# The first feed-forward product of a hybrid decoder by Strassen's algorithm, its result kept in fp32

## The chip, the cores and the metric

The kernel runs on one core of a Trainium2 chip, in one launch. The metric is the device time of that core in microseconds (us), the median over several executions. The engines are named as in the profile: PE (TensorE, matmuls), PEld (its weight loads), DVE (VectorE), ACT (ScalarE), POOL (GpSimd) and SP (SyncE, which issues the DMAs).

## The reference

One inference step of a decoder with two layers, D = 1024 features, over 576 tokens (512 of a prompt and 8 sequences of 8). Each layer is

```
x <- LN(alpha*x + 0.5*SwiGLU_1(x))
x <- LN(alpha*x + W_out(gated sum of four mixing branches of x))
x <- LN(alpha*x + 0.5*SwiGLU_2(x))
SwiGLU(x): gate, up = split(x @ w_in); (silu(gate) * up) @ w_out
```

`w_in` is 1024 x 4096 (2048 gate columns, 2048 up columns) and `w_out` 2048 x 1024, all in fp32. There are four feed-forward layers (FFN), two in each layer. The four branches (RWKV, pooling, gated delta rule, attention into a memory) and their states lie between the two FFNs of a layer; the change doesn't touch them.

## The kernel before, in words

**Numbers.** Every dense product is done in three passes: an fp32 operand is split into a high part (a cast to fp32r) and a low part (the difference). A weight piece of 128 x 4 x 128 comes by a DMA of 256 KB into `raw`, ACT casts it into `w[:, 0]` (line 232), DVE subtracts into `w[:, 1]` (line 234); `unit` does this for a piece of n x 128 rows. x, h and the like are split by `split` (lines 261 and 262), in the same two steps. `mms` (line 248) issues for each 128 rows of the contraction high x high, high x low and low x high: three matmuls of 128x128 weights and 288 tokens.

**Tokens.** Features lie on the partitions, tokens along the free axis, in two halves of 288 (`HALVES`). x is held split, in eight tiles `X`.

**One FFN** (`ffn`): 16 blocks j of 128 hidden columns. A block takes two units of weights (gate, up) and, for each half s, two products of 8 x 3 = 24 matmuls into PSUM (`pg`, `pu`); then ACT makes silu(gate), DVE multiplies by up (line 433), and `split` writes the result as `H[j]`. The second product (`out_norm`) runs over 8 output blocks with all 16 H, 48 matmuls a half, in pieces of 4 x 3 matmuls; the second half of the tokens follows the first 3 pieces behind, and the first half does the last 8 pieces at once. Then comes the residual (DVE, line 281, onto T_j, which POOL made from the two parts of x, line 274), the sums for the norm, and `layer_norm` in steps: a small chain on DVE, two products with ones (`prow`), and for each block a multiplication (DVE, line 352), an addition (POOL, line 353), scale and bias (ACT), and the split into X. The first half's norm lies beside the end of the second half's products; the second half's norm (`finish_norm`) is left to what follows, and the next FFN does three blocks of the first half meanwhile.

**The mixing's output product** goes through `out_norm` as well, with 8 operand tiles instead of 16: 24 matmuls for a block and half.

**Order.** The code is traced in Python and a scheduler places the instructions on each engine's queue by their order in the code and by when they can start; on the chip each engine runs its queue in order, and waits are semaphores. Tiles with the same tag share a fixed number of slots (`BUFS`): 8 of "x", 8 of "s", 4 of "d", 3 of "p", 2 of "iv", 4 of "w" and 4 of "wm" (weights), 3 and 3 for `raw`. PSUM has two banks for each of the tags "mm" and "mg" of these products.

Of the kernel before, what the change touches and what calls it, by code (L numbers as in the profile page):

```python
# [15 lines left out]
P = 128  # L16
# [3 lines left out]
NS = 8          # sample sequences  # L20
LS = 8          # tokens of each
# [4 lines left out]
NC_ = 9         # chunks of 64 tokens: 8 of the prompt, one of the sample group  # L26
# [24 lines left out]
# rows of 128 parameters, in two groups that one transpose each brings onto the partitions  # L51
# [5 lines left out]
# how the work that fills the tensor engine's gaps in the token mixing is laid between the rest: its order at first  # L57
# (P: pooling and attention, G: gates of the first merge), how many steps of it go where, and how many columns of an
# inverse lie between two steps
ORDER = "P" * 11 + "GP" * 16  # L60
PLAN = (12, 0, 4, 0, 12, 8, 0, 0, 2, 0, 4, 4, 0, 2)
RWKV_EVERY, DELTA_EVERY = 3, 8


class Decoder:
# [45 lines left out]
    def tri(self, t, strict, block=None):  # L111
        """t[s, j] (square in the last two dims of a [n, n] tile): 1 where s <= j (s < j if strict) else 0."""
# [5 lines left out]
    def blockdiag(self, t, b):  # L118
        """zero outside the b x b diagonal blocks of t [n, m]."""
# [8 lines left out]
    def constants(self):  # L128
# [11 lines left out]
        # inclusive upper triangles, by chunk of 64 and by sequence of 8  # L140
# [6 lines left out]
        # seqmask[t, b] = 1 where token t (mod 64) belongs to sequence b  # L147
# [3 lines left out]
        # masks of the RWKV token x token matrices [s | s, t strict | t inclusive]  # L151
# [10 lines left out]
        # 0 where s <= t else NEG: [128 = (h, s), 2 kinds, 64]  # L162
# [5 lines left out]
        # stacked identity [128 = (h, s), 64]  # L168
        self.id2 = c.tile([P, 64], F32, name="id2")
        nc.vector.tensor_add(self.id2, self.ident[:, 0:64], self.ident[:, 64:128])  # L170
        # rows 4 r + g of the identity on the partitions (.., g, 8 matrices): [128, 8, 32]
# [8 lines left out]
        # 0 at the first token of a chunk or sequence, else 1  # L180
# [6 lines left out]
        # 1 / (t + 1)  # L187
# [4 lines left out]
    def params(self, l):  # L192
        """parameters of a layer, feature on partition, one column for each block of 128."""
# [27 lines left out]
    def unit(self, src):  # L221
        """a [128, n, 128] piece of a weight, n <= 8, as high and low parts: tiles [128, 2, 4, 128]."""
# [28 lines left out]
    def stash(self, k, src, sl=slice(0, NT)):  # L251
        """rows k (of 14 blocks) of the branches' outputs, to DRAM."""
        dst = self.od[k][:, sl]
        if len(src.shape) == 3:
            dst = dst.rearrange("p (c t) -> p c t", t=src.shape[2])
        self.nc.sync.dma_start(dst, src)
# [1349 lines left out]
```

## Time and profile before

| | |
|---|---|
| median of three runs | 3292.2 us (3291.89 to 3294.51) |
| profiled execution, its span | 3291.1 us, 62683 instructions |
| the profiled execution's own time | not given beside the span |
| PE busy | 3164.5 us, 96%, 24736 matmuls |
| DVE busy | 1896.7 us, 58% |
| ACT busy | 1276.8 us, 39% |
| POOL busy | 581.2 us, 18% |
| DMA | 271.96 MB, mean 83 GB/s |

Busy time of PE is that of pipelined instructions, whose ends are modelled: 24 matmuls one behind the other show as one row that is a little longer than the distance to the next. The span's clock is 0.974 of the upper level in the mean. The four FFNs lie at about 22 to 337, 1325 to 1644, 1644 to 1960 and 2952 to 3269 us.

### The profile page before, as it was taken

How to read it: one execution, taken by the hardware profiler on the slowest of the kernel's cores; microseconds unless marked ns; L12 is line 12 of the kernel's file. 1: busy time of each engine (PE TensorE's matmuls, PEld its weight loads, DVE VectorE, ACT ScalarE, POOL GpSimd, SP SyncE). 2: the span in 40 equal slices, each digit the busy share in tenths (PEclk: the TensorE clock that was granted, in tenths of full speed). 3: DMA queues.
4: the chain of work that ended last, by engine and by line, in shares of the span. 5: the costliest groups of instructions: out<-in, count | busy, mean ns of one | idle time of the engine just before them, and what ended most of it. 6: DMA issues, size and time to landing. Idle time of an engine off the chain costs nothing. (4 is left out here: it accounts for less than half of the span.)

```text
span 3291.1 us, 62683 instructions
## 1 busy us (share of the span) xinstructions
PE 3164.5 (96%) x24736; PEld 2886.2 (88%) x24736; DVE 1896.7 (58%) x4205; ACT 1276.8 (39%) x3015; POOL 581.2 (18%) x898
## 2 busy tenths in 40 slices
PE   7999999999999999999999999998999999999998
PEld 7999887688888799999999998776888797989998
DVE  5336676465677656733663376675475786475336
ACT  4323544434434233432343244444345342343324
POOL 2002311111110014400330032111111100152004
PEclk8999899999999899999999999999999998999999
DMA  4223331142233233332333232312322232323222
GB/s 137 80 84 96 87 111 44 41 118 55 60 83 78 57 105 91 91 87 80 88 103 87 81 107 72 105 51 55 102 58 61 67 99 64 98 85 97 84 81 77
DMA packets 509908, 271.96 MB, mean 83 GB/s; under 512 B 45897, under 2 KB 500141, under 8 KB 509613
## 3 DMA queue, kind: packets, MB, share of 16 engines
q1 hardware_dynamic: 509612, 267.95, 29.0%
q8 instruction: 194, 3.18, 0.4%
q14 instruction: 102, 0.83, 0.1%
HBM read 248.12 MB, written 19.76 MB: 81 GB/s over the span
## 5 line engine op out<-in xcount | busy, mean ns | idle before, releaser
L234 DVE TENSOR_TENSOR w<-raw,w 128x512 fp32r<-128x512 f32 (+1 forms) x824 | 604.7, 739 | 385.2 <-ACT w L232 378.0
L232 ACT CAST w<-raw 128x512 fp32r<-128x512 f32 (+1 forms) x824 | 501.6, 615 | 608.8 <-PE po L248 236.4
L248 PE MATMUL pp<-X,w 128*128 128x288 f32 x3552 | 550.9, 307 | 11.1 <-DVE X L262 5.5
L248 PEld LDWEIGHTS pp<-X,w 128*128 128x128 f32 x3552 | 495.1, 193 | 40.1 <-issue 15.3
L248 PE MATMUL pgt<-X,w 128*128 128x288 f32 x3072 | 500.9, 309 | 5.1 <-ACT th__12080 L1484 2.1
L248 PEld LDWEIGHTS pgt<-X,w 128*128 128x128 f32 x3072 | 435.1, 193 | 32.6 <-issue 13.9
L248 PE MATMUL pg<-X,w 128*128 128x288 f32 x3072 | 441.8, 297 | 10.2 <-DVE X L262 6.1
L248 PE MATMUL pu<-X,w 128*128 128x288 f32 x3072 | 437.4, 297 | 0.0
L248 PEld LDWEIGHTS pg<-X,w 128*128 128x128 f32 x3072 | 419.7, 189 | 15.7 <-DVE X L262 9.6
L248 PEld LDWEIGHTS pu<-X,w 128*128 128x128 f32 x3072 | 420.9, 190 | 0.6
L248 PE MATMUL po<-H,w 128*128 128x288 f32 x3072 | 413.9, 296 | 0.0
L248 PEld LDWEIGHTS po<-H,w 128*128 128x128 f32 x3072 | 409.4, 188 | 1.3
L248 PE MATMUL pbr<-O,w 128*128 128x288 f32 x1344 | 227.6, 308 | 12.9 <-ACT w L232 4.1
L248 PEld LDWEIGHTS pbr<-O,w 128*128 128x128 f32 x1344 | 190.9, 191 | 27.9 <-issue 7.3
L276 POOL TENSOR_TENSOR T<-T,m 128x288 f32<-128x288 f32 x48 | 48.0, 1029 | 925.7 <-ACT m L297 925.4
L433 DVE TENSOR_TENSOR h<-h,pu 128x288 f32<-128x288 f32 x128 | 58.0, 453 | 259.2 <-PE pu L248 259.1
L261 ACT CAST H<-h 128x288 fp32r<-128x288 f32 x128 | 55.2, 431 | 189.5 <-DVE h L433 189.4
L432 ACT ACTIVATE h<-pg 128x288 f32<-128x288 f32 x128 | 52.7, 411 | 172.8 <-PE pg L248 172.8
L248 PE MATMUL po<-mh,w 128*128 128x288 f32 x768 | 109.0, 302 | 9.2 <-DVE T L281 9.2
L248 PEld LDWEIGHTS po<-mh,w 128*128 128x128 f32 x768 | 105.6, 193 | 11.4 <-DVE T L281 6.9
L614 DVE TENSOR_TENSOR it<-W,iu 128x60 f32<-128x60 f32 (+24 forms) x372 | 97.7, 263 | 9.2
L353 POOL TENSOR_TENSOR T<-T,off 128x288 f32<-128x288 f32 x96 | 83.4, 900 | 91.5 <-ACT off L348 65.0
(1018 smaller groups left out, 3747.8 us busy)
## 6 DMA issues: line engine op xcount, KB each, us to landing
raw<-in_w_in_dram SPq DMA_DIRECT2D x280, 256.0 KB
raw<-in_ffn_w_in_dram SPq DMA_DIRECT2D x272, 256.0 KB
raw<-in_ffn_w_out_dram SPq DMA_DIRECT2D x160, 256.0 KB
raw<-in_w_branch_dram SPq DMA_DIRECT2D x48, 256.0 KB
raw<-in_w_out_dram SPq DMA_DIRECT2D x48, 256.0 KB
oraw<-od SPq DMA_DIRECT2D x28, 288.0 KB
kraw<-in_mem_w_kv_dram SPq DMA_DIRECT2D x16, 256.0 KB
kvr<-in_cache_mem_k_dram SPq DMA_DIRECT2D x16, 256.0 KB
```

What stands on the lines that cost most here:

```text
L232: nc.scalar.copy(w[:, 0, :m], raw)
L234: low.tensor_sub(w[:, 1, :m], raw, w[:, 0, :m].bitcast(F32))
L248: self.nc.tensor.matmul(ps, w[:, wp, d, :], X[k][:, part, sl], start=first and k == 0 and q == 0, stop=last and k == n - 1 and q == 2)
L261: nc.scalar.copy(out[:, 0, sl], src)
L276: nc.gpsimd.tensor_sub(t, t, self.stat[s]['m'])
L353: nc.gpsimd.tensor_add(T[j], T[j], off)
L432: nc.scalar.activation(h, pg, AF.Silu)
L433: nc.vector.tensor_mul(h, h, pu)
L614: nc.vector.tensor_mul(w, d[:, :r, k:k + 1].to_broadcast([P, r, m]), u[:, k + 1:, k].unsqueeze(1).to_broadcast([P, r, m]))
```

## The change

The first product of each FFN is computed as a 2 x 2 block product with seven block products instead of eight (Winograd's form). The contraction is cut in two (four blocks of 128 features each), the tokens in their two halves (B11, B21: the first half's x; B22 and T1 to T4: the second half's x and differences of both), the columns in gate and up. `seven` makes the operands, as the layer norm (or `load_x`, at the start) delivers x: for the first half the same splits as before; for the second, when blocks 4 to 7 come, two subtractions on DVE, two on POOL and five splits for each pair of blocks. For each block of columns `sums` makes four sums of the weights on POOL, and `parts` splits seven pieces: two for `first` (the first half's gate, and x's part that all share), five for `rest`. Each product is 4 x 3 = 12 matmuls; DVE combines them from PSUM into `h`, which is kept in fp32. Six blocks' `first` are done ahead, beside the second half's norm; their weights are loaded again later. x itself stays in fp32 in T, as the residual. The second product then runs in two passes over 8 hidden blocks each: `h` is split into H for the pass; the first pass adds its products onto T, the second goes through `out_norm` with 8 tiles. The output of the norm goes to a hook: `plain` (split into X, before the mixing) or `seven` (before an FFN).

Comments and blank lines are left out, and renamed arguments of `out_norm` and `layer_norm`.

```diff
@@ -264,24 +265,25 @@
     def wview(self, name, l):
         return self.i[name][l].rearrange("(k p) c -> p k c", p=P)
     def addend(self, j, s):
         nc, sl = self.nc, HALVES[s]
-        if s == 0 and j % 2 == 0:
+        if self.base and s == 0 and j % 2 == 0:
             self.T.append(self.slot("T", tag="o"))
         t = self.T[j // 2][:, j % 2, sl]
-        nc.gpsimd.tensor_add(t, self.X[j][:, 0, sl].bitcast(F32), self.X[j][:, 1, sl].bitcast(F32))
+        if self.base:
+            nc.gpsimd.tensor_add(t, self.base[j][:, 0, sl].bitcast(F32), self.base[j][:, 1, sl].bitcast(F32))
         if j > 3:
...
@@ -352,13 +354,53 @@
             nc.vector.tensor_mul(T[j], T[j], rows[0])
             nc.gpsimd.tensor_add(T[j], T[j], off)
             nc.scalar.activation(T[j], T[j], AF.Identity, bias=b[:, c:c + 1], scale=g[:, c:c + 1])
-            if not final:
-                self.split(self.X[j], T[j], sl)
-    def out_norm(self, units, X, which, lag, ahead, final=False):
-        self.T, self.stat = [], [{}, {}]
+            out(j, s)
+    def plain(self, j, s):
+        if s == 0:
+            if j == 0:
+                self.X = []
+            self.X.append(self.slot("X", F32R, tag="x"))
+        self.split(self.X[j], self.T[j // 2][:, j % 2, HALVES[s]], HALVES[s])
+    SEVEN = (("B11", "d"), ("B21", "d"), ("T2", "x"), ("T1", "x"), ("T4", "x"), ("B22", "x"), ("T3", "iv"))
+    def seven(self, j, s):
+        nc = self.nc
+        if j == 0:
+            if s == 0:
+                self.B = {}
+            for name, tag in self.SEVEN[:2] if s == 0 else self.SEVEN[2:]:
+                t = [self.slot(name, F32R, [P, 2, 2, HT], tag) for _ in range(2)]
+                self.B[name] = [t[k // 2][:, k % 2] for k in range(4)]
+        x = lambda i, h: self.T[i // 2][:, i % 2, HALVES[h]]
+        whole = slice(0, HT)
+        if s == 0:
+            self.split(self.B["B21" if j > 3 else "B11"][j % 4], x(j, 0), whole)
+        elif j > 3:
+            k = j - 4
+            t1, t2 = self.half("t1"), self.half("t2")
+            nc.vector.tensor_sub(t1, x(k, 1), x(k, 0))
+            nc.vector.tensor_sub(t2, x(j, 1), t1)
+            self.split(self.B["T2"][k], t2, whole)
+            self.split(self.B["T1"][k], t1, whole)
+            nc.gpsimd.tensor_sub(t1, t2, x(k, 0))
+            nc.gpsimd.tensor_sub(t2, x(j, 0), t2)
+            self.split(self.B["T3"][k], t1, whole)
+            self.split(self.B["T4"][k], t2, whole)
+            self.split(self.B["B22"][k], x(j, 1), whole)
+    def out_norm(self, units, X, which, lag, ahead, out):
+        self.base = self.X
+        if self.base:
+            self.T = []
+        self.stat = [{}, {}]
         per = len(X) // 4
         n = 8 * per
         loaded, ps, due = {}, {}, [None, None]
...
@@ -403,60 +445,123 @@
         self.norm = self.layer_norm(1, *prm)
     def finish_norm(self):
         for _ in self.norm or ():
             pass
         self.norm = None
-    def ffn(self, l, w_in, w_out, which, final=False):
+    def quarter(self, src):
+        raw = self.raw("raw", 512).rearrange("p (k c) -> p k c", c=P)
+        self.nc.sync.dma_start(raw, src)
+        return raw
+    def parts(self, raw):
+        nc = self.nc
+        tag = self.wtags[self.wi % len(self.wtags)]
+        self.wi += 1
+        w = self.slot("w", F32R, [P, 2, 4, P], tag)
+        nc.scalar.copy(w[:, 0], raw)
+        nc.vector.tensor_sub(w[:, 1], raw, w[:, 0].bitcast(F32))
+        return [(w, d) for d in range(4)]
+    def ffn(self, l, w_in, w_out, which, out):
         nc = self.nc
         wi, wo = self.wview(w_in, l), self.wview(w_out, l)
-        H = []
-        tags = ["d"] * 4 + ["p"] * 3 + ["iv"] + ["s"] * 8
         self.wtags = ("w", "wm")
-        def weights(j):
-            if len(H) <= j:
-                H.append(self.slot("H", F32R, [P, 2, NT], tags[j]))
-            return [self.unit(wi[:, :, c:c + P]) for c in (j * P, FF + j * P)]
-        def step(j, s, u):
-            sl = HALVES[s]
-            pg = self.dense("mm", "pg")
-            self.mms(pg, u[0], self.X, sl)
-            pu = self.dense("mg", "pu")
-            self.mms(pu, u[1], self.X, sl)
-            h = self.half("h")
-            nc.scalar.activation(h, pg, AF.Silu)
-            nc.vector.tensor_mul(h, h, pu)
-            self.split(H[j], h, sl)
-        step(0, 0, weights(0))
-        u = [weights(1), weights(2)]
-        self.finish_norm()
-        step(1, 0, u[0])
-        step(2, 0, u[1])
-        step(1, 1, u[0])
-        step(2, 1, u[1])
-        step(0, 1, weights(0))
-        for j in range(3, 16):
-            u = weights(j)
-            for s in range(2):
-                step(j, s, u)
-        self.out_norm(lambda j, kh: wo[:, kh * 8:kh * 8 + 8, j * P:(j + 1) * P], H, which, 3, 8, final)
+        whole = slice(0, HT)
+        h = []
+        def at(j, s):
+            if len(h) <= j // 2:
+                h.append(self.slot("h"))
+            return h[j // 2][:, j % 2, s * HT:(s + 1) * HT]
+        def piece(i, k, j):
+            c = i * FF + j * P
+            return self.quarter(wi[:, 4 * k:4 * k + 4, c:c + P])
+        def first(j, u11, u12):
+            ps = self.dense("mm", "p1")
+            self.mms(ps, u11, self.B["B11"], whole)
+            nc.scalar.copy(at(j, 1), ps)
+            ps = self.dense("mg", "p2")
+            self.mms(ps, u12, self.B["B21"], whole)
+            nc.vector.tensor_add(at(j, 0), at(j, 1), ps)
+            nc.scalar.activation(at(j, 0), at(j, 0), AF.Silu)
+        def sums(a11, a12, a21, a22):
+            S = [self.slot("S", F32, [P, 2, 4, P], "p") for _ in range(2)]
+            s1, s2, s3, s4 = S[0][:, 0], S[0][:, 1], S[1][:, 0], S[1][:, 1]
+            nc.gpsimd.tensor_add(s1, a21, a22)
+            nc.gpsimd.tensor_sub(s2, s1, a11)
+            nc.gpsimd.tensor_sub(s3, a11, a21)
+            nc.gpsimd.tensor_sub(s4, a12, s2)
+            return s1, s2, s3, s4
+        def rest(j, a22, s1, s2, s3, s4):
+            def product(w, name, tag):
+                ps = self.dense(tag, name)
+                self.mms(ps, self.parts(w), self.B[name], whole)
+                return ps
+            u2, u3, u4 = self.half("u2"), self.half("u3"), self.half("u4")
+            nc.vector.tensor_add(u2, at(j, 1), product(s2, "T2", "mm"))
+            nc.vector.tensor_add(u3, u2, product(s3, "T3", "mg"))
+            p5 = product(s1, "T1", "mm")
+            nc.vector.tensor_add(u2, u2, p5)
+            nc.vector.tensor_add(u4, u3, p5)
+            nc.vector.tensor_add(u3, u3, product(a22, "T4", "mg"))
+            nc.vector.tensor_mul(at(j, 0), at(j, 0), u3)
+            nc.vector.tensor_add(u2, u2, product(s4, "B22", "mm"))
+            nc.scalar.activation(u2, u2, AF.Silu)
+            nc.vector.tensor_mul(at(j, 1), u2, u4)
+        for j in range(EARLY):
+            first(j, *[self.parts(piece(0, k, j)) for k in range(2)])
+            if j == 2:
+                self.finish_norm()
+        for j in range(16):
+            a21, a22, a11, a12 = [piece(i, k, j) for i, k in ((1, 0), (1, 1), (0, 0), (0, 1))]
+            S = sums(a11, a12, a21, a22)
+            if j >= EARLY:
+                first(j, self.parts(a11), self.parts(a12))
+            rest(j, a22, *S)
+        self.X = None
+        n = 8
+        for g in range(2):
+            H = []
+            for j in range(n):
+                H.append(self.slot("H", F32R, [P, 2, NT], "x" if g == 0 else ("s", "s", "s", "s", "p", "p", "p", "iv")[j]))
+                self.split(H[j], h[(g * n + j) // 2][:, j % 2, :NT], slice(0, NT))
+            units = lambda j, kh: wo[:, g * n:g * n + n, j * P:(j + 1) * P]
+            if g == 0:
+                for j in range(8):
+                    u = self.unit(units(j, 0))
+                    for s in range(2):
+                        ps = self.dense(("mm", "mg")[s], "po")
+                        self.mms(ps, u, H, HALVES[s])
+                        self.residual(j, s, ps)
+        self.out_norm(units, H, which, 3, 8, out)
         self.wtags = ("w",)
     def load_x(self):
-        nc = self.nc
-        self.X = [self.slot("X", F32R, tag="x") for _ in range(8)]
+        nc = self.nc
+        self.T = [self.slot("T", tag="o") for _ in range(4)]
         for t in range(5):
             if t == 3:
+                for j in range(8):
+                    self.seven(j, 0)
                 yield
             n = P if t < 4 else NS * LS
             src = self.i['x_prompt'][0, t * P:t * P + n] if t < 4 else self.i['x_sample'].rearrange("b t d -> (b t) d")
@@ -468,8 +573,10 @@
                     nc.tensor.transpose(pt[:, j * P:j * P + n], xr[:n, j * P:(j + 1) * P], self.ident[:n, :n])
                 for j in range(4):
                     k, sl = g * 4 + j, slice(t * P, t * P + n)
-                    nc.scalar.copy(self.X[k][:, 0, sl], pt[:, j * P:j * P + n])
-                    nc.vector.tensor_sub(self.X[k][:, 1, sl], pt[:, j * P:j * P + n], self.X[k][:, 0, sl].bitcast(F32))
+                    (nc.scalar.copy if j % 2 else nc.vector.tensor_copy)(self.T[k // 2][:, k % 2, sl],
+                                                                         pt[:, j * P:j * P + n])
+        for j in range(8):
+            self.seven(j, 1)
     def store_y(self):
         nc = self.nc
...
@@ -1571,7 +1678,7 @@
                 self.split(H[j], self.M[j // 2][:, j % 2, sl], sl)
         wo = self.wview('w_out', l)
         self.wtags = ("w", "wm")
-        self.out_norm(lambda j, kh: wo[:, :, j * P:(j + 1) * P], H, 1, 3, 8)
+        self.out_norm(lambda j, kh: wo[:, :, j * P:(j + 1) * P], H, 1, 3, 8, self.seven)
         self.wtags = ("w",)
```

## Rows read from the trace of the kernel before

**Rows 1.** The page's first part: busy us (share of the span) xinstructions.

```profile
PE 3164.5 (96%) x24736; PEld 2886.2 (88%) x24736; DVE 1896.7 (58%) x4205; ACT 1276.8 (39%) x3015; POOL 581.2 (18%) x898
```

**Rows 2.** The page's groups: line, engine, operation, count | busy, mean | idle.

```profile
L248 PE MATMUL pg<-X,w 128*128 128x288 f32 x3072 | 441.8, 297 | 10.2 <-DVE X L262 6.1
...
L248 PE MATMUL po<-H,w 128*128 128x288 f32 x3072 | 413.9, 296 | 0.0
```

**Rows 3.** Timeline, TensorE, main loop: start us, duration, instruction, count [idle].

```profile
1382.90 3.36 PE L248 MATMUL pu<-X,w 128*128 128x288 f32 x24
1386.10 3.32 PE L248 MATMUL pg<-X,w 128*128 128x288 f32 x24
1389.26 3.32 PE L248 MATMUL pu<-X,w 128*128 128x288 f32 x24
```

**Rows 4.** Windows: length, busy by engine (instructions), clock, DMA share, GB/s.

```profile
1360.00:1538.00 178.00, 178.00 (x1345) 178.00 (x1344) 67.50 (x116) 57.85 (x116) 7.62 (x7) 1.00 0.31 90
...
1324.70:1343.00 18.30, 16.75 (x111) 15.82 (x110) 16.53 (x42) 12.41 (x26) 6.21 (x7) 0.91 0.30 88
1343.00:1356.30 13.30, 11.59 (x77) 10.43 (x76) 11.76 (x18) 9.10 (x21) 12.60 (x15) 0.96 0.06 19
...
22.70:41.00 18.30, 17.13 (x113) 16.10 (x114) 13.34 (x32) 11.20 (x30) 6.45 (x8) 0.87 0.72 210
...
1261.90:1324.70 62.80, 56.96 (x406) 54.98 (x404) 48.49 (x86) 21.50 (x43) 38.60 (x40) 0.97 0.35 102
...
231.00:337.00 106.00, 105.88 (x796) 105.22 (x795) 61.59 (x107) 34.32 (x66) 25.24 (x28) 1.00 0.31 90
```

**Rows 5.** Timeline, start of an FFN, second half's layer norm.

```profile
1342.81 2.64 DVE L352 TENSOR_TENSOR T<-T,prow 128x288 f32<-128x288 f32 x7 [0.55 <-PE prow L345]
...
1351.91 0.66 PE L248 MATMUL pg<-X,w 128*128 128x288 f32 x3 [0.28 <-DVE X L262]
...
1356.24 4.50 PE L248 MATMUL pu<-X,w 128*128 128x288 f32 x24
```

**Rows 6.** Waits, TensorE, mixing's output product: us in total, times, longest.

```profile
PE po L248 <- DVE T L281: 4.6, 4, 2.0
```

**Rows 7.** Timeline: operations queued back to back; GpSimd beside the second.

```profile
342.49 3.70 DVE L234 TENSOR_TENSOR w<-raw,w 128x512 fp32r<-128x512 f32 x6 [0.40 <-ACT w L232]
...
354.49 2.64 DVE L352 TENSOR_TENSOR T<-T,prow 128x288 f32<-128x288 f32 x7 [0.54 <-PE prow L345]
...
355.45 5.08 POOL L353 TENSOR_TENSOR T<-T,off 128x288 f32<-128x288 f32 x6 [7.69 <-ACT off L348]
```

**Rows 8.** Groups by shape, ScalarE, main loop of one FFN (as rows 2).

```profile
L232 ACT CAST w<-raw 128x512 fp32r<-128x512 f32 x60 | 37.1, 619 | 35.1 <-PE pu L248 15.4 <-ACT w L232 10.1 <-PE pg L248 8.9
...
L432 ACT ACTIVATE h<-pg 128x288 f32<-128x288 f32 x28 | 11.5, 412 | 42.1 <-PE pg L248 42.1
```

**Rows 9.** Groups by shape, GpSimd, whole span (as rows 2).

```profile
L917 POOL TENSOR_TENSOR ex<-VS,seqm 128x512 f32<-128x512 f32 x16 | 16.4, 1044 | 27.2 <-ACT VS L832 27.2
```

**Rows 10.** Timeline: GpSimd alone, GpSimd and VectorE at once, VectorE alone.

```profile
37.85 6.51 POOL L274 TENSOR_TENSOR T<-X 128x288 f32<-128x288 f32 x8 [11.77 <-DVE X L472]
...
1286.04 3.90 POOL L276 TENSOR_TENSOR T<-T,m 128x288 f32<-128x288 f32 x4 [9.77 <-ACT m L297]
...
1286.22 4.03 DVE L301 TENSOR_TENSOR T<-T,m 128x288 f32<-128x288 f32 x4
...
318.00 0.81 POOL L309 TENSOR_TENSOR s<-s,T 128x288 f32<-128x288 f32 x1 [5.55 <-DVE T L281]
318.05 1.31 DVE L234 TENSOR_TENSOR w<-raw,w 128x512 fp32r<-128x512 f32 x1 [0.19 <-ACT w L232]
...
319.65 0.69 DVE L234 TENSOR_TENSOR w<-raw,w 128x512 fp32r<-128x512 f32 x1
```

**Rows 11.** Timeline, VectorE, main loop: order of a split and a multiplication.

```profile
1385.40 0.69 DVE L234 TENSOR_TENSOR w<-raw,w 128x512 fp32r<-128x512 f32 x1 [0.65 <-ACT w L232]
1386.30 0.46 DVE L433 TENSOR_TENSOR h<-h,pu 128x288 f32<-128x288 f32 x1 [0.21 <-PE pu L248]
```

More of the change, by code (lines that the diff above doesn't have):

```diff
@@ L62 @@
 RWKV_EVERY, DELTA_EVERY = 3, 8
+EARLY = 6
 class Decoder:
@@ L320, in rsqrt, with layer_norm @@
             nc.vector.scalar_tensor_tensor(y, t, 1.5, y, ALU.add, ALU.mult)
-    def layer_norm(self, s, which, final, g, b):
+    def layer_norm(self, s, which, out, g, b):
         nc, sl, st = self.nc, HALVES[s], self.stat[s]
@@ L394, in out_norm @@
             step(i, 0)
-        prm = (which, final, self.p['ln_g'], self.p['ln_b'])
+        prm = (which, out, self.p['ln_g'], self.p['ln_b'])
         norm = self.layer_norm(0, *prm)
@@ L499, in run @@
             self.params(l)
-            self.ffn(l, 'ffn1_w_in', 'ffn1_w_out', 0)
+            self.ffn(l, 'ffn1_w_in', 'ffn1_w_out', 0, self.plain)
             self.mixing(l)
-            self.ffn(l, 'ffn2_w_in', 'ffn2_w_out', 2, final=l == DEPTH - 1)
+            self.ffn(l, 'ffn2_w_in', 'ffn2_w_out', 2, self.seven if l < DEPTH - 1 else lambda j, s: None)
         self.wtags = ("w", "wm")
```

## Prediction

> **What bounds the kernel now.** I began with the page: TensorE (PE) is busy for 96% of the span [rows 1], so what counts is how many matmuls there are and where PE waits. The groups of instructions come next: pg, pu and po, the feed-forward (FFN) products, are 9216 of its 24736 instructions [rows 2]. The timeline of PE in the main loop of one FFN then gives the price: bursts of 24 matmuls start 3.20 and 3.16 us apart with no idle time, so 0.1325 us per 128x288 matmul, at the clock's upper level [rows 3, 4]. (The 295 ns in the groups are pipelined durations and no cost.) In that loop VectorE (DVE) and ScalarE (ACT) are busy for a good third and GpSimd (POOL) has little to do [rows 4]. So fewer matmuls are time won, as long as no other engine comes up to PE. Last I looked at where PE does wait around an FFN: at its start, for the second half's x, and in the mixing's output product, for DVE [rows 4 to 6].
>
> **Matmuls removed.** A block of 128 hidden columns takes 2 x 2 products of 24 matmuls, 96; by seven half-depth products of 12 it takes 84. 12 x 16 blocks x 4 FFNs = 768 matmuls, x 0.1325 = -101.8 us. The second product keeps its 768 matmuls per FFN, in two passes.
>
> **What a block asks of the others.** PE: 84 x 0.1325 = 11.1 us (before 12.7). DVE: seven weight splits instead of four, and nine 128x288 operations. Queued back to back a split takes 3.70 / 6 = 0.62 us and a 128x288 operation 2.64 / 7 = 0.38 [rows 7]: 4.3 + 3.4 = 7.7 us. ACT: seven casts of 0.62, a copy and two Silu of 0.41 [rows 8]: 5.6 us, hidden. POOL: four 128x512 sums, new. The nearest rows are 1.04 us for a 128x512 operation (one operand broadcast) and 0.81 for 128x288 alone, by elements 1.44 [rows 9, 10]: 4.2 to 5.8 us. None alone reaches 11.1.
>
> **But DVE and POOL hold each other up.** Alone, a 128x288 addition takes POOL 0.81 us; four of them beside four DVE subtractions ran in step, 3.90 and 4.03 us for four [rows 10], so a pair costs some 1.02 us and POOL's addition takes 1.02 - 0.38 = 0.64 us from DVE. Below, "of the pair" is time that only one of the two can use. A weight split beside a 0.81 us POOL addition took 1.31 us instead of 0.69, the same 0.6 [rows 10]. DVE operations that read PSUM are not held up: seven in 2.64 us, with POOL at work [rows 7]. The Trainium skill ("SBUF — State Buffer", section "SBUF: two separate sides") has a stricter rule: an exclusive lock for the whole instruction, the loser blocked. By it the pair would cost 0.45 + 0.81 = 1.26 us; the row's 1.02 disagrees in size and agrees in kind, and the row decides. For 128x512 no row shows the loss: at least 0.64 + (1.04 - 0.81) = 0.87, at most 0.64 x 512/288 = 1.14; I take 1.0, between.
>
> **Steady blocks (7 to 16 of each FFN).** DVE operations with two SBUF inputs, 7 x 0.62 + 2 x 0.38 = 5.1, and POOL's share 4 x 1.0: 9.1 us; the seven that read PSUM add 2.6 if none runs beside POOL. 9.1 to 11.7 against PE's 11.1, and eight weight tiles in stock even it out. 40 such blocks: +8 us for queueing (0.2 each); bounds 0 and, with 1.14 and nothing hidden, 1.1 x 40 = 44.
>
> **Start of an FFN.** Before, after the second half's layer norm, 8 splits of x end the wait. Now x's blocks 4 to 7 also make T1 to T4 and B22: 20 splits and 8 subtractions on DVE, 8 more on POOL beside the norm's 8 additions. That is 28 x 0.38 + 16 x 0.64 = 20.9 us of the pair. PE meanwhile has the six early pairs of products (2 x 12 matmuls, 3.2 us each), as long as the three blocks it had before (19.1). And then the first six blocks are short on PE, 60 matmuls or 7.95 us, while they want 5 x 0.62 + 2 x 0.38 + 4 x 1.0 = 7.9 of the pair, +2.3 on PSUM. From the norm's rows (at 1342.8 [rows 5]) PE has some 48 matmuls and six short blocks left, 54.1 us. The pair has 20.9 + 3.7 (six early splits) + 6 x 7.9, less six sums that the S tiles can take ahead: 66 us; the PSUM work is 17.7 more, hidden from all to none. I take all hidden, because in 1343 to 1356.3 the 15 POOL additions and nine subtractions alone account for 15 x 0.64 + 9 x 0.38 = 13.0 of 13.3 us, though the norm's eight PSUM operations ran too (window in [rows 4], 15 instructions on POOL and 18 on DVE). So PE is some 12 us short, 2.7 of which it loses there now (77 matmuls and little else in 13.3 us [rows 4]): +9 net. Four starts (the first has no norm but nothing lost now): +36 us. Bounds: -11 (the present loss goes too) and, with 1.14 and nothing hidden, 29 x 4 = 116.
>
> **First seam.** The splits of the kept products need the x slots, free with the last block's products: 8 x 0.69 (576 columns) on DVE, most in its idle quarter or under the first 3.2 us of the next product: +2 each, 8 us; bounds 0 and 5.5 x 4 = 22. The other eight are ready through a pass of 51 us in which DVE has 27 of work: nothing, 22 if they wait for the end of it. That instructions move ahead of their place in the code is seen where a split for the next weights runs ahead of the multiplication that ends the last block [rows 11].
>
> **Second pass.** Its loop, eight units with 24 matmuls a piece, is that of the mixing's output product: there PE is busy 56.96 of 62.80 us, in the FFN's present one 105.88 of 106 [rows 4]; 4.6 us are waits for DVE's residual [rows 6], behind four subtractions that alternate with POOL's. +5 each, 20 us; bounds 0 and 5.7 x 4 = 23.
>
> **Loads.** Each FFN loads 8 pieces of 256 KB more (12 early ones again for 4). The short blocks want 1 MB per 8 us (132 GB/s), and the start of the kernel ran at 210 [rows 4]: hidden; if the queue stands behind a piece not yet released, up to 1 us in each of 24 short blocks. POOL's 64 additions x = high + low go; they are off the path.
>
> **Sum** against the profiled execution (3291.1 us of span, nothing else known around it, 1.1 under the median): -101.8 + 8 + 36 + 8 + 20 = -30, so 3261, and 3262 as a median.
>
> **Rivals.**
> - *POOL's sums make DVE the bound (slower).* Place: the start and the six short blocks. If the PSUM operations don't hide beside POOL, a start lacks 9 + 17.7 u, u the share not hidden; the whole is -102 + 36 + 71 u + 36, which turns positive from u = 0.42. At u = 1 it is +26 with 0.87 for the loss (start 24 each, steady blocks 3) and +86 with 1.14 and the steady blocks' 44: 3317 to 3377, 3335 as one number. For it: pairs in step [rows 10]. Against: the 13.3 us window. If a POOL operation took its whole time from DVE, 0.81 and 1.44, a start would lack 76 - 57 = 19 us even with the PSUM work hidden: -102 + 78 + 36 = +12, 3303, and this rival would begin there; I give that 0.05 of its chance, since the pairs show 0.64. It is what the lock rule of the Trainium skill ("SBUF — State Buffer", section "SBUF: two separate sides") would make of this kernel.
> - *All is covered.* Early products and weight tiles stocked ahead hide the start and the blocks; the second pass stays: -102 + 20 = 3210. For it: PE runs without a gap through all the main loop [rows 3]. Against: the layer norm's end is late already now [rows 5].
> - *The gain is eaten.* A start costs 14, not 9, and the clock falls after such waits: it was 0.91 and 0.96 of the upper level in the two windows of a start [rows 4], where 24 matmuls took 4.50 us, not 3.32 [rows 3, 5]. 4 x (5 + 2) more: 3290.
> - *The seven products run one by one,* each split waiting for the sum of the product before: five times 0.45 + 0.69 in 64 blocks is +365, some 3555. The order in [rows 11] speaks against it.
>
> **Chances.** Forecast (3228 to 3284) 0.45, all covered (under 3228) 0.16, eaten (3285 to 3299) 0.15, DVE bound 0.21, one by one 0.03. The range, 3210 to 3330, leaves out the last, the upper end of DVE bound, and a little below. What can be told from no change is 0.2%, 6.6 us: faster 0.61, same 0.15, slower 0.24. Within the likeliest case alone, 3228 to 3284.
>
> **What would show it.** In the profile after: PE with 23968 instructions; bursts of 12 with under 0.3 us idle in the later blocks (steady blocks right); weight splits well over 0.74 us in the mean, beside POOL sums of 1.0 to 1.5; 10 to 15 us of PE idle between the last early product and the fourth block, put down to DVE; 5 us in the second pass. Wrong, if the later blocks come over 11.8 us apart (DVE bound), if PE idles at the seams, or if the short blocks run at 8 us.

## The result

The kernel after takes 3372.8 us (median of 4, 3366.5 to 3381.6), the kernel before beside it 3292.1 (3288.8 to 3294.5): a ratio of 1.0244, 95% interval 1.0224 to 1.0264. The change makes it slower by 81 us; 3262 was forecast.

The matmuls went as they should (24736 in [rows 1], 23968 now), and everything else grew. First the page of the kernel after:

```profile
PE 3113.1 (92%) x23968; PEld 2817.3 (83%) x23968; DVE 2383.0 (71%) x4905; ACT 1402.4 (41%) x3235; POOL 951.1 (28%) x1122
...
L249 PE MATMUL T<-T,w 128*128 128x288 f32 x3072 | 432.4, 300 | 41.1 <-DVE u L518 22.3
...
L249 PE MATMUL po<-H,w 128*128 128x288 f32 x3072 | 422.1, 299 | 8.7 <-DVE T L283 8.7
...
L249 PE MATMUL p<-B,w 128*128 128x288 f32 x1536 | 241.9, 315 | 71.6 <-ACT w L466 36.4
...
L467 DVE TENSOR_TENSOR w<-S,w 128x512 fp32r<-128x512 f32 x256 | 271.3, 1061 | 20.8 <-ACT w L466 17.7
...
L467 DVE TENSOR_TENSOR w<-raw,w 128x512 fp32r<-128x512 f32 x192 | 178.8, 941 | 11.6 <-ACT w L466 11.6
...
L501 POOL TENSOR_TENSOR S<-S,raw 128x512 f32<-128x512 f32 x64 | 87.7, 1370 | 166.2 <-DMA raw<-in_ffn_w_in_dram 165.7
```

p is the two quarter-products of `first` (the early ones among them), T the four with T1 to T4, po the second product; the seventh, with B22, has a group of its own that idles for nothing. Where pg idled for 10.2 us and po for none [rows 2], p, T and po now idle for 121. The place is best seen stage by stage. These are the windows of the second FFN, in the columns of [rows 4]: from the first early product to the first T product, the six short blocks, the ten later ones, the second product.

```profile
1342.00:1391.30 49.30, 28.89 (x161) 26.16 (x159) 39.37 (x80) 28.48 (x62) 22.47 (x24) 0.72 0.19 54
1391.30:1453.00 61.70, 50.43 (x360) 48.20 (x361) 61.25 (x83) 23.27 (x42) 43.85 (x29) 1.00 0.40 116
1453.00:1564.50 111.50, 111.50 (x842) 111.50 (x841) 107.60 (x168) 57.94 (x112) 49.77 (x34) 1.00 0.35 100
1564.50:1679.50 115.00, 108.47 (x790) 106.75 (x789) 71.50 (x129) 34.68 (x67) 26.10 (x26) 0.97 0.28 82
```

At 0.1325 us a matmul the stages need 19.1, 47.7, 111.3 and 101.8 us. So the start loses 30 us, a short block 2.3 us, the later blocks nothing, although DVE is busy in 107.60 of their 111.50 us; and the second product, 105.88 busy of 106 before [rows 4], takes 9 to 10 us longer. The granted clock of 0.72 in the start stands beside the stops: PE idles for 20.4 of the 49.3 us there; in the blocks after it the granted clock is 1.00.

By the timelines of the two profiled executions the four first products take 881.3 us instead of 849.1 (+32.2, although 101.8 of matmuls are gone), the four second products 461.6 instead of 421.8 (+39.8), all else 2036.9 instead of 2020.2 (+16.7): 88.7 in all, for spans of 3379.7 and 3291.1. Of the last 16.7, 14.0 stand in the second mixing (1000.9 us for 986.9; the first: 990.6 for 988.3). The other kernels with two passes and 8 pieces (e1 to e4, e6, e9, e14) had 989 to 999 and once 1003.5, so part of these may belong to this execution, which is 8.7 us over its kernel's median; I did not find their place.

**In the start** PE's waits (us in total, times, longest; 1341 to 1455) are for the weights of early products:

```profile
PE p L249 <- ACT w L466: 10.1, 1, 10.1
PE p L249 <- DVE w L467: 6.7, 2, 5.4
PE T L249 <- DVE u L518: 6.7, 3, 3.4
```

The timeline shows why the cast was late (start us, duration, engine, line, tile; L391 and L392 are POOL's subtractions for the operands, L262 ACT's casts and L263 DVE's remainders of them, L466 and L467 the same for a weight):

```profile
1365.71 1.86 PE L249 MATMUL p<-B,w 128*128 128x288 f32 x13
...
1370.45 0.87 POOL L391 TENSOR_TENSOR t<-t,T 128x288 f32<-128x288 f32 x1 [1.99 <-DVE T L263]
1371.36 0.43 ACT L262 CAST T<-t 128x288 fp32r<-128x288 f32 x1 [0.32 <-POOL t L391]
...
1374.72 0.43 ACT L262 CAST T<-t 128x288 fp32r<-128x288 f32 x1 [1.64 <-POOL t L391]
...
1377.03 1.13 ACT L466 CAST w<-raw 128x512 fp32r<-128x512 f32 x2
...
1377.69 0.85 PE L249 MATMUL p<-B,w 128*128 128x288 f32 x2 [10.12 <-ACT w L466]
...
1384.18 1.28 DVE L467 TENSOR_TENSOR w<-raw,w 128x512 fp32r<-128x512 f32 x2
1384.92 5.17 PE L249 MATMUL p<-B,w 128*128 128x288 f32 x20 [5.40 <-DVE w L467]
...
1389.33 1.27 POOL L501 TENSOR_TENSOR S<-S,raw 128x512 f32<-128x512 f32 x1 [6.11 <-DMA raw<-in_ffn_w_in_dram]
...
1391.30 0.53 PE L249 MATMUL T<-T,w 128*128 128x288 f32 x2 [1.22 <-ACT w L466]
```

Each engine works through its queue in order. Here the last early products' weights stand in ACT's and DVE's queues behind the making of the seven operands; ACT waits there for POOL's subtractions, POOL for DVE's remainders. PE stops at 1367.6 with 24 early matmuls left. When these weights are split at last, their raw buffer comes free, the load of block 0's next piece starts, POOL waits 6.11 us for it, and only then come the sum, its cast and the first T product. The wait of the load's issuer, SP, for such a split is in the waits of 1341 to 1453:

```profile
SPq L457 <- DVE w L467: 48.7, 10, 18.6
```

### The profile page after: what moved, and what is told of

Same layout as the page of the kernel before. It is cut to its first block, busy times and chain, and to the rows that moved or that the text cites. A ratio compares the mean times of both kernels' runs of the same rounds, so it can differ in the third digit from the quotient of the medians.

```text
span 3379.7 us, 62780 instructions
## 1 busy us (share of the span) xinstructions
PE 3113.1 (92%) x23968; PEld 2817.3 (83%) x23968; DVE 2383.0 (71%) x4905; ACT 1402.4 (41%) x3235; POOL 951.1 (28%) x1122
## 5 line engine op out<-in xcount | busy, mean ns | idle before, releaser
L249 PE MATMUL pp<-X,w 128*128 128x288 f32 x3552 | 549.6, 306 | 16.7 <-ACT pa L635 8.8
L235 DVE TENSOR_TENSOR w<-raw,w 128x512 fp32r<-128x512 f32 (+1 forms) x552 | 402.7, 734 | 186.5 <-ACT w L233 182.2
L233 ACT CAST w<-raw 128x512 fp32r<-128x512 f32 (+1 forms) x552 | 334.7, 612 | 466.2 <-PE po L249 261.4
L249 PE MATMUL T<-T,w 128*128 128x288 f32 x3072 | 432.4, 300 | 41.1 <-DVE u L518 22.3
L249 PEld LDWEIGHTS T<-T,w 128*128 128x128 f32 x3072 | 418.7, 191 | 50.2 <-ACT w L466 28.6
L249 PE MATMUL p<-B,w 128*128 128x288 f32 x1536 | 241.9, 315 | 71.6 <-ACT w L466 36.4
L249 PEld LDWEIGHTS p<-B,w 128*128 128x128 f32 x1536 | 226.3, 204 | 80.2 <-ACT w L466 39.0
L467 DVE TENSOR_TENSOR w<-S,w 128x512 fp32r<-128x512 f32 x256 | 271.3, 1061 | 20.8 <-ACT w L466 17.7
L466 ACT CAST w<-S 128x512 fp32r<-128x512 f32 x256 | 154.8, 618 | 130.3 <-POOL S L501 52.1
L467 DVE TENSOR_TENSOR w<-raw,w 128x512 fp32r<-128x512 f32 x192 | 178.8, 941 | 11.6 <-ACT w L466 11.6
L466 ACT CAST w<-raw 128x512 fp32r<-128x512 f32 x192 | 117.6, 619 | 79.8 <-PE B L249 29.9
L283 DVE SCALAR_TENSOR_TENSOR T<-po,T 128x288 f32<-128x288 f32 x160 | 72.1, 452 | 92.8 <-PE po L249 92.5
L500 POOL TENSOR_TENSOR S<-raw 128x512 f32<-128x512 f32 x64 | 100.8, 1575 | 73.6 <-DMA raw<-in_ffn_w_in_dram 34.1
```

Source lines behind the costliest of these rows:

```text
L233: nc.scalar.copy(w[:, 0, :m], raw)
L235: low.tensor_sub(w[:, 1, :m], raw, w[:, 0, :m].bitcast(F32))
L249: self.nc.tensor.matmul(ps, w[:, wp, d, :], X[k][:, part, sl], start=first and k == 0 and q == 0, stop=last and k == n - 1 and q == 2)
L283: self.nc.vector.scalar_tensor_tensor(t, ps, RES, t, ALU.mult, ALU.add)
L466: nc.scalar.copy(w[:, 0], raw)
L467: nc.vector.tensor_sub(w[:, 1], raw, w[:, 0].bitcast(F32))
```

## Experiments

Three theories. **A:** POOL's sums hold DVE up, so the short blocks are bound by DVE. **B:** the start is bound by queue order and buffers. **C:** the last pass of the second product puts the first half's norm where the second half's mean is being taken out. In us, medians and ratios to the kernel before measured beside each (3292.1 to 3294.0), 95% interval; e4, e9 and e14 leave out work that the result needs:

| run | median | ratio | against after |
|---|---|---|---|
| after | 3372.8 | 1.0244 [1.0224, 1.0264] | |
| e1 sums on DVE | 3329.8 | 1.0101 [1.0076, 1.0126] | -43.0 |
| e2 separate turns | 3342.5 | 1.0149 [1.0127, 1.0171] | -30.4 |
| e3 norm interleaved | 3365.7 | 1.0218 [1.0199, 1.0237] | -7.1 |
| e4 no sums | 3304.3 | 1.0035 [1.0024, 1.0045] | -68.5 |
| e5 ten pieces | 3344.8 | 1.0162 [1.0133, 1.0190] | -28.0 |
| e6 = e1 + e2 | 3307.2 | 1.0041 [1.0026, 1.0056] | -65.7 |
| e7 = e1 + e2 + e3 + e5 | 3290.1 | 0.9993 [0.9983, 1.0002] | -82.7 |
| e8 = e7, 8 early blocks | 3288.8 | 0.9981 [0.9968, 0.9994] | -84.0 |
| e9 four operands left out | 3336.3 | 1.0134 [1.0115, 1.0153] | -36.5 |
| e10 one pass | 3314.6 | 1.0061 [1.0045, 1.0076] | -58.2 |
| e11 = e8, subtractions on DVE | 3278.6 | 0.9955 [0.9943, 0.9968] | -94.3 |
| e12 = e11 in one pass | 3242.3 | 0.9846 [0.9831, 0.9861] | -130.5 |
| e13 = e12, block 0's sums on POOL | 3259.6 | 0.9899 [0.9883, 0.9916] | -113.3 |
| e14 = e2 + e9 | 3321.6 | 1.0092 [1.0071, 1.0113] | -51.3 |

And by stage, from the timelines: first early product to first T product + first T to first po product; the second product. The first FFN has no norm of a half before it, the second has one. The two parts of a first product are to be read as one sum: what shortens the start can come back in the blocks.

| run | first FFN | second FFN | second product |
|---|---|---|---|
| PE's work (after) | 19.1 + 159.0 | 19.1 + 159.0 | 101.8 |
| PE's work (8 early) | 25.4 + 152.6 | 25.4 + 152.6 | 101.8 |
| before | 209.1 | 213.2 | 105.5, 105.4 |
| after | 40.8 + 172.8 | 49.4 + 173.2 | 115.6, 115.2 |
| e1 | 40.0 + 162.9 | 46.3 + 163.9 | 114.6, 114.7 |
| e2 | 29.2 + 179.3 | 36.0 + 178.2 | 115.4, 114.5 |
| e3 | 40.5 + 172.3 | 43.2 + 177.2 | 114.5, 114.7 |
| e4 | 39.7 + 159.4 | 36.7 + 167.4 | 115.3, 114.2 |
| e6 | 37.6 + 161.4 | 41.0 + 166.1 | 115.7, 113.0 |
| e9 | 27.1 + 176.6 | 36.1 + 176.8 | 114.6, 115.0 |
| e14 | 23.9 + 178.2 | 34.1 + 174.0 | 115.5, 114.5 |
| e10 | 40.6 + 172.7 | 47.5 + 173.1 | 105.4, 105.7 |
| e12 (8 early) | 41.6 + 155.2 | 45.1 + 167.4 | 105.3, 105.4 |

**e1, the sums on DVE; e4, no sums.**

```diff
-            nc.gpsimd.tensor_add(s1, a21, a22)
+            nc.vector.tensor_add(s1, a21, a22)
...
# e4, in place of the four sums:
+            s1, s2, s3, s4 = a21, a11, a21, a12
```

> The four fp32 sums of each block move from POOL to DVE; nothing else changes. Theory A (POOL's sums hold DVE up: w<-S subtractions of 0.95 to 1.18 us that take 0.72 us in the kernel before): a short block's DVE work falls from 10.2 to about 9 us although four sums of about 0.6 us are added, a later block's from 10.8 to about 10.5; about -32 us, near 3340. Rival (DVE has too much of its own work, POOL beside it costs little): 2.4 us more in each block, short blocks 12.6 us and later ones 13.2 instead of 11.15; about +140 us, near 3510. Theory B (the order of the queues at an FFN's start): no change at the start, the stall between the early products and the first T product stays at about 30 us.

> The four sums are left out (their consumers read the raw blocks instead), so POOL has no work in a block. Theory A: short blocks fall from 10.3 us to PE's 8.0, DVE's w subtractions to about 0.7 us: -14 us per FFN, and the way to the first T product loses two sums, -3: about -65 to -70, near 3305. Theory B alone: short blocks stay at about 10 us since they wait for DVE's own work, -10 to -15 in all.

e1 gave -43.0 (forecast by A -32, by its rival +140), e4 -68.5 (forecast -65 to -70). Theory A is shown for the short blocks: with more operations on it, DVE gets through them sooner. In the first FFN the 13.8 us above PE's 159.0 fall to 3.9 with the sums on DVE and to 0.4 without them. The groups of DVE by shape, in the short blocks of the second FFN, say how; first the kernel after, then e1:

```profile
L467 DVE TENSOR_TENSOR w<-S,w 128x512 fp32r<-128x512 f32 x27 | 31.9, 1184 | 6.1 <-ACT w L466 5.8
L467 DVE TENSOR_TENSOR w<-raw,w 128x512 fp32r<-128x512 f32 x9 | 9.4, 1047 | 0.0
L520 DVE TENSOR_TENSOR h<-h,u 128x288 f32<-128x288 f32 x6 | 6.3, 1055 | 0.2
L523 DVE TENSOR_TENSOR h<-u,u 128x288 f32<-128x288 f32 x5 | 4.4, 886 | 0.0
L514 DVE TENSOR_TENSOR u<-h,T 128x288 f32<-128x288 f32 x6 | 2.6, 441 | 0.0
```

```profile
L467 DVE TENSOR_TENSOR w<-S,w 128x512 fp32r<-128x512 f32 x24 | 16.0, 686 | 0.0
L500 DVE TENSOR_TENSOR S<-raw 128x512 f32<-128x512 f32 x6 | 4.1, 687 | 0.0
```

Beside POOL a split takes 1184 ns instead of 686, the multiplications of two SBUF operands 1055 and 886 instead of 452 and 454 (e1); an operation that reads PSUM (L514) keeps its 441. That is 27 x 0.50 + 9 x 0.36 + 6 x 0.60 + 5 x 0.43 = 22.5 us for 24 sums, 0.94 us of DVE per sum.

In the start neither run helps the first FFN (40.8, 40.0, 39.7), as theory B said of e1. In FFNs with a norm e4 shortens it by 13 us, which was not forecast, and 8 us above PE's work stay in the blocks there (167.4).

**e2, separate turns; e3, the norm interleaved; e6.** Loading and splitting advanced one shared counter, so loads always fell on one kind of raw buffer (3 of 6) and splits on one kind of split buffer (4 of 8).

```diff
# e2
+        self.qi += 1
-        raw = self.raw("raw", 512).rearrange("p (k c) -> p k c", c=P)
+        raw = self.raw("raw", 512, "r" + self.wtags[self.qi % 2]).rearrange("p (k c) -> p k c", c=P)
# e3
-            if j == 2:
-                self.finish_norm()
+            for _ in range((0, 0, 2, 3, 3, 0)[j]):
+                next(self.norm or iter(()), None)
+        self.finish_norm()
```

> Loads and splits take turns over both kinds of buffer separately (6 raw and 8 split buffers for a feed-forward's weights, where a shared counter had given 3 and 4). Theory B (buffers and queue order): block 0's loads no longer wait for a raw buffer, the 6 us wait of POOL for a DMA before the first sums goes; -5 to -8 us per FFN, about 3345 to 3350. Theory A (DVE and POOL together): nothing, 3373 within 5 us.

> The second half's norm and the seven operands are issued in three portions between early products 2 to 5 instead of all of them behind product 2, so that the casts of products 3 to 5 stand ahead of part of it in ACT's and DVE's queues. Theory B: PE's wait of 10.1 us for a cast and most of the 5.4 us after it go in the three FFNs that have a norm there, -10 to -15 us each, about 3330 to 3343. Theory A: the work of the seven operands only ends later, the first T product too; within 8 us of 3373.

> The sums on DVE and the separate turns of buffers together, measured alone at -43 and -30 us. If the two act on different stretches (short blocks; the start), they add: near 3300. If both take away the same wait (POOL's sums late behind a load), 3325 to 3330.

e2 did more than forecast for the start (-12 and -13 us), and PE's longest wait in it (1338 to 1440) is another:

```profile
PE p L249 <- ACT h L492: 5.7, 1, 5.7
PE T L249 <- ACT w L467: 4.7, 2, 4.0
```

But the blocks give back 5 to 6.5 us of that per FFN; DVE is busy in 60.97 us of the first 65.50 of them (1374.50 to 1440). e3 missed theory B's forecast and lies within the rival's 8 us: PE's wait of 10.1 us goes, but its waits for the weights of early products only fall from 16.8 to 12.8 us (in the second FFN, longest 6.8), and the blocks give back 4 of the 6 us that the start gains. So another order in the code does not free the start by itself. e1 and e2 together give 65.7 of the 73.4 us that they give alone, nearly separate in the whole; not by stage, for in e6 the first FFN's start is 37.6 us where e2 had 29.2, and its blocks 161.4 where e2 had 179.3.

**e9 and e14, the operands' work.**

```diff
-            nc.vector.tensor_sub(t1, x(k, 1), x(k, 0))
...
-            self.split(self.B["B22"][k], x(j, 1), whole)
+            self.split(self.B["T2"][j - 4], x(j, 1), whole)
+            # T1, T4, B22, T3: the same buffer as T2
```

> The making of four of the seven operands is left out (T1, T3, T4 and B22 are the buffer of T2, and that holds a plain split of x): of 7 DVE, 5 ACT and 2 POOL operations per pair of tiles one ACT and one DVE operation remain. Theory B (the early products' weights and the first T product stand behind the making of the operands): PE's waits among the early products go, the start falls from 41 to 51 us to 23 to 28 us, -60 to -90 in all, near 3295. Rival (the start waits for the loads of block 0, which have 3 raw buffers): no more than the 6 us of that wait in the FFN's start is left to gain or lose, the start stays above 35 us, above 3345.

> Separate turns of the buffers, with four of the seven operands left out as before. Alone each took the start of an FFN with a norm from about 49 to 36 us. If they are two separate causes, the start falls to 24 to 27 us (21.7 is PE's work there with the load of its first operands), 3336 - 30 = about 3306. If one had been hidden behind the other all along, 33 to 36 us and about 3330.

Both forecasts missed. Alone, the missing operands shorten the start by 13.7 and 13.3 us, no more than the buffers do, and -36.5 us is half of what I expected. Together the two bring the first FFN's start to 23.9 (forecast 24 to 27), but one with a norm only to 34.1. So buffers and operands are links of one chain, and breaking either frees most of it; about 10 us of a start with a norm are neither. The first FFN, which has no norm there, doesn't show them (23.9 against 34.1), so I put them down to that norm; no run leaves it out.

**e5, ten pieces; e10, one pass.**

```diff
# e5 (and the same for the mixing's out product)
-        self.out_norm(units, H, which, 3, 8, out)
+        self.out_norm(units, H, which, 3, 10, out)
# e10
-        for g in range(2):
...
+        for j in range(16):
+            H.append(self.slot("H", F32R, [P, 2, NT], (["x"] * 8 + ["s"] * 4 + ["p"] * 3 + ["iv"])[j]))
+            self.split(H[j], h[j // 2][:, j % 2, :NT], slice(0, NT))
```

> In the second product's last pass (and the mixing's out product) the first half's last 10 pieces are done at once instead of 8, so that the norm of the first half is issued two pieces earlier, ahead of the second half's mean (4 subtractions on POOL and 4 on DVE). Theory C (PE's wait of 4.3 us for the norm's diagonal comes from the collision of the two: the chain of 13 small operations on DVE takes 11 us beside the mean's subtractions and 3.1 us in the kernel before): prow's wait falls below 1.5 us, -3 to -5 us per FFN and -2 per mixing, about -20, near 3353. Rival (two passes cost their own, whatever the order: shorter units, splits of H late): second product stays at 115 us, 3373 within 4.

> The second product in one pass again, over 16 tiles of H split at the seam (in the kernel before they were split block by block). Theory C (the second pass puts the second half's mean and the first half's norm in one place): its end is as in the kernel before, prow's wait under 1.5 us; -6 to -10 per FFN there, against a seam of 4 to 10 us while the splits of H (0.75 us on DVE each) stay behind PE; so 3345 to 3375. Rival (the 10 us come from the clock or from units of 8 pieces and are there anyway): prow's wait stays near 4 us and the time rises by the seam, 3385 to 3410.

In the kernel after, the norm's chain of small DVE operations (lnw) starts at 1660.30, stands among the mean's subtractions and sums of the second half, and lets PE go on at 1671.72 (timeline):

```profile
1659.85 5.97 POOL L278 TENSOR_TENSOR T<-T,m 128x288 f32<-128x288 f32 x4 [5.04 <-ACT m L299]
...
1660.30 0.16 DVE L335 TENSOR_SCALAR lnw<-pv 96x6 f32<-96x6 f32 x1 [1.18 <-PE pv L331]
...
1671.22 0.82 DVE L343 TENSOR_TENSOR dg<-ident,lnw 96x288 f32<-96x288 f32 x2
...
1671.72 2.29 PE L347 MATMUL prow<-dg,ones 96*128 96x288 f32 x4 [4.32 <-DVE dg L343]
```

The chain has 11 us where it had 3.1 in the kernel before. (dg is the diagonal that prow multiplies with ones.) e5 takes prow's wait away there, as C says, but the stop moves: PE then waits up to 4.3 us for a residual (T L283). e5's second product stays at 115 us and more, as the rival said; its -28.0 comes from the stage after it, whose early products now begin before the last po: from the second FFN's first po product to the third's it is 332.1 us, 339.6 in the kernel after.

By the code the collision comes from the lead: 8 pieces were two output blocks and are four in a pass of half the depth, so that the first half's norm is issued when the second half stands at block 2, ahead of the mean (behind block 3), where it stood at block 5 before. A lead of 4 pieces would keep the old order; no run tried it.

e10 shows that the 10 us are the price of the second pass, and not of the clock or of units of 8 pieces, which e10 has too: its second product takes 105.3 to 106.0 us, as before, here in the window's columns, and in the groups po idles for none again:

```profile
1548.70:1654.40 105.70, 105.57 (x791) 104.53 (x789) 68.25 (x118) 37.26 (x72) 27.00 (x29) 1.00 0.30 89
```

```profile
L249 PE MATMUL po<-H,w 128*128 128x288 f32 x3072 | 413.6, 296 | 0.0
```

I had feared a seam of 4 to 10 us for its 16 splits; there is none that PE shows. The gain is larger than forecast (-58.2, not 0 to -28): 40 us in the second products, and the rest in what follows them. After a two-pass FFN the next stage also starts late. PE's waits around the seam to the first mixing, in the kernel after (335 to 400) and in e10 (325 to 390):

```profile
PE prow L347 <- DVE dg L343: 5.1, 2, 4.5
PE pp L249 <- ACT pa L635: 4.4, 1, 4.4
```

```profile
PE pp L249 <- DVE X L263: 2.8, 5, 1.3
...
PE prow L347 <- DVE dg L343: 0.5, 2, 0.3
```

(The 4.5 of the first row is still the second product's.)

**All together: e7, e8, e11, e12, e13.**

```diff
# e8, e11 to e13
-EARLY = 6
+EARLY = 8
# e11 to e13
-            nc.gpsimd.tensor_sub(t1, t2, x(k, 0))
-            nc.gpsimd.tensor_sub(t2, x(j, 0), t2)
+            nc.vector.tensor_sub(t1, t2, x(k, 0))
+            nc.vector.tensor_sub(t2, x(j, 0), t2)
# e13
+            S = sums(nc.gpsimd if j == 0 else nc.vector, a11, a12, a21, a22)
```

> Sums on DVE, separate turns, the 10 pieces, and the norm issued between the early products. If all four causes are separate: 3373 - 43 - 30 - 20 - 7 = about 3273, faster than before by 0.6%. If they overlap, 3290 to 3310 and no gain on before.

> As the run with all four, with 8 early blocks for 6: 6.4 us more of PE's work beside the making of the seven operands, at the price of two more short blocks. Theory B (the start is now bound by the amount of work of the operands, about 27 us on DVE, against 19 us of early products): -4 to -6 us per FFN, less 1.3 us of loss in the short blocks, -12 to -18 against the run with six, near 3258. Rival (the start is bound by the order in the queues, in which the first T product's split comes last): the T product moves back by the same time, 0 within 5.

> All four edits with 8 early blocks (3289 us when POOL still made two of the operands' subtractions), and these subtractions on DVE too. Theory A for the start (POOL's SBUF operations hold DVE's up: a split of 0.44 us takes 1.04 us beside one): 8 DVE operations of 0.45 us more, 8 to 16 that are 0.6 us shorter, and no hand-over between engines: -3 to -6 us per FFN, near 3272, faster than before by 0.6%. Rival (DVE is the bound of the start by its own work): +2 to +3.6 us per FFN, near 3300.

> The seven products with every repair: sums and all of the seven operands' subtractions on DVE, separate turns of the buffers, 8 early blocks with the norm between them, the mixing's 10 pieces, and the second product in one pass. If the second pass's price (10.0 us per FFN in the run with one pass) is apart from the others: 3278.6 - 40 = 3239, and part of what the 10 pieces gave is lost again, so 3235 to 3255. If the overlaps had already taken it: 3265 to 3280.

> As the run before, with the sums of block 0 on POOL. Theory B (DVE is full until the first T product, and POOL idle): the first T product comes up to 2.4 us sooner in each FFN, 0 to -10. Rival (POOL's sums hold DVE's subtractions up here too): 0 to +6.

e7 is no faster than before: the four overlap by 26 us. Two more early blocks (e8) are worth nothing that can be told from it, as the rival said; DVE then has two more short blocks. Taking the operands' subtractions off POOL (e11) gave -10 against e8, where A forecast -17 and its rival a loss; but the second FFN's start stays (43.4 and 43.5 us), and the gain stands in the blocks behind it (171.9 and 169.3). One pass (with 8 pieces there again, 10 in the mixing) gave another -36 (e12, in its forecast of 3235 to 3255). **e12 is 1.5% faster than the kernel before**, so the seven products do pay once the three prices are off. In the table it seems to gain only in the first FFN, because its early products begin 14 us before the mixing's last matmul; from the last matmul of one second product to the first of the next it takes 1190.3, 204.5 and 1188.6 us for 1201.5, 214.0 and 1200.0 before. One of its edits, the mixing's ten pieces, could be made in the kernel before too and was not tried there; the first and third FFN, which it doesn't touch, gain 13 and 10 us each. Its groups show the splits at their own speed:

```profile
L468 DVE TENSOR_TENSOR w<-S,w 128x512 fp32r<-128x512 f32 x256 | 171.4, 684 | 2.7 <-ACT w L467 2.3
```

It is still 52 us above the 3190 that the matmuls alone would give (3292 - 101.8). e13 lost 17 us, beyond both of its forecasts: four sums put back on POOL meet the norm's chain, as this timeline shows, and PE's wait for that chain (prow for dg, second FFN) is 5.7 us where e12 has 1.8.

```profile
1325.85 0.16 DVE L322 SCALAR_TENSOR_TENSOR lnw<-lnw 96x3 f32<-96x3 f32 x1
...
1327.23 1.59 POOL L502 TENSOR_TENSOR S<-S,raw 128x512 f32<-128x512 f32 x1
1327.63 1.21 DVE L320 SCALAR_TENSOR_TENSOR lnw<-lnw 96x3 f32<-96x3 f32 x1
...
1328.79 1.26 POOL L503 TENSOR_TENSOR S<-raw 128x512 f32<-128x512 f32 x1
1329.13 0.94 DVE L321 TENSOR_TENSOR lnw<-lnw 96x3 f32<-96x3 f32 x1
...
1330.02 1.26 POOL L504 TENSOR_TENSOR S<-raw,S 128x512 f32<-128x512 f32 x1
1330.10 1.19 DVE L322 SCALAR_TENSOR_TENSOR lnw<-lnw 96x3 f32<-96x3 f32 x1
```

## Why the prediction was wrong

**Right:** the matmuls (-101.8), and that a POOL sum costs DVE about 1.0 us (0.94 measured). The later blocks (+8 foreseen) and the first seam (+8) cost nothing: po starts without a gap behind the last block.

**The start, +36 foreseen, about +134 measured** (101.8 + 32.2 over four FFNs, 33.5 each). Even the step's upper bound, 116, was too low. Two sentences of it failed.

- "I take all hidden." In the short blocks DVE is busy in 61.25 of 61.70 us: its PSUM operations are not slowed by POOL, but they stand in one queue with the splits that are, so their time adds. At u = 1 the working gave 7.9 + 2.3 = 10.2 us per block; 10.3 was measured. The window from which I took u = 0 had DVE busy in 11.76 of 13.3 us: it showed the two running at once, not that a full queue could hide anything. This is the place and the price of the rival that I gave 0.21 (3317 to 3377), without the steady blocks' part of it. That the measured time lies inside that range is partly luck: the rival put up to 44 us on the later blocks, which cost nothing, and it had neither the stall below nor the second pass's full price.
- "From the norm's rows PE has some 48 matmuls and six short blocks left." This balanced PE's work against the pair's over the whole start, as if either could always go on with the next piece. PE could not: its early weights were queued behind the operands, with 3 raw and 4 split buffers in use (the working counted on eight), so it stood idle for 20.4 of 49.3 us with short blocks still to come. The edit that touches the buffers alone (e2) takes 12 to 15 us off a start, of which the blocks give back 4 to 6.5; the order of the code alone (e3) takes 6, and 4 come back.

"Loads: hidden" fell with it: not for bandwidth (54 GB/s in that window) but for want of a free buffer.

**The second pass, +20 foreseen, 40 measured.** I sized it by the mixing's output product, which has the same loop, and took its waits for the residual. The new waits were the norm's chain against the second half's mean (4.3 of some 10 us) and residuals (2.1 us; how the rest divides is open), plus what the later norm holds up behind the pass; going back to one pass returned 58 us. The remaining +16.7 outside the FFNs' products had no term.

Of the signs it named, two came: slow weight splits (1061 and 941 ns in the mean against "well over 0.74") and later blocks at PE's own pace (11.15 us each). The wait at the start was put down to ACT first, where I had named DVE.

## What to carry to other kernels

Two engines' work may be balanced as one sum only if neither waits for the other inside it: for a start, write down each queue in order and ask which instruction the idle engine's next work stands behind, and which buffer its load needs. On an engine that is busy throughout (DVE here, 61.25 of 61.70 us) nothing is hidden; its operations add, slowed ones and others alike. And when a loop's units are halved, look again at every lead that is counted in units.

## What the hardware showed

A small DVE operation on SBUF that starts beside a POOL operation ends with it: in e13, operations of 0.16 us took 1.21, 0.94 and 1.19 us, and ended at 1328.84, 1330.07 and 1331.29, POOL's at 1328.82, 1330.05 and 1331.28. Of the 50 steps of this chain with two SBUF inputs that began with more than 0.05 us of a POOL operation still to run, in the kernel after and in e13, 47 ended 13 to 23 ns after it. The Trainium skill ("SBUF — State Buffer", section "SBUF: two separate sides") says just this of a DVE operation with two SBUF inputs, as these have, beside a POOL operation that reads SBUF: the one that starts first holds the shared port for its whole instruction, and the other is blocked. The trace agrees. The prediction had set that rule below its row of 1.02 us per pair. Over the short blocks the loss is 0.94 us per sum of 1.3 to 1.7, less than the whole; DVE spends part of each sum on operations that read PSUM, which keep their 441 ns.

POOL's 128x512 addition of two full operands took 1.27 us where nothing else showed beside it and up to 1.86 beside DVE; the nearest row before, with one operand broadcast, was 1.04 [rows 9].
